# First block: values projected before the norm's statistics are known, projections woven between the softmax steps

## The chip, the cores and the metric

The kernel runs on one core of a Trainium2 chip. The metric is the device time of one execution in microseconds; three runs of the kernel before lie between 2774.18 and 2778.89, with a median of 2776.5.

## What is computed

The whole program is one hybrid block on 256 tokens of width 1024, followed by four further layers (gated linear attention, a conformer convolution, grouped-query attention, gated linear attention again), each with an MLP. The change lies at the very start of the first block. Cut to that part, the reference is:

```
xn = rmsnorm(x, norm1_w)                       # x * rsqrt(mean(x^2) + eps) * norm1_w
q, k, v, z, xbc, dt_raw, gate_logits = split(xn @ w_in)
# 24 heads of 64 in 3 dilated groups of 8, blocks of 128 queries, 256 keys
logits = q k^T / 8 + bias ;  masked where the key is out of the window
p = exp(logits - max) / sum                    # softmax; the 3 groups are merged
attn = p v                                     # by a softmax over all three together
merged = sigmoid(gate0) * (attn @ w_attn_branch) + sigmoid(gate1) * (ssm @ w_ssm_branch)
```

All arithmetic is float32. The weight products are made from three products each: a number is split into a rounded part "hi" and a rest "lo", and hi·hi, hi·lo and lo·hi are added up.

## The kernel before

**Weights.** Weights come in units. `Unit` loads a unit from HBM on SyncE's queue in chunks of 128x1024 floats (512 KB) into `wraw` (3 buffers), ScalarE rounds the chunk into `whi`, and VectorE takes the rest into `wlo` (5 buffers each, line 435). A projection (`fm2`) makes one unit of two chunks (four for the values) and then its 48 products through `mm3` (line 456): TensorE loads one operand and streams 256 columns of the other (512 for the values).

**Order.** The program is written as one sequence. A planner spreads it over the engines at build time. It keeps the written order where it can, but lets a later instruction go ahead on an engine when by its own estimates the earlier ones aren't ready. On the chip each engine then works its list strictly in that fixed order. So the load of the conditions (`conditions`, written after the keys) is issued at 9.18 us, and the sums of `decay_sums`, written after the fourth key unit, run between 28 and 52 us.

**Start.** x arrives, ScalarE squares it (line 408), VectorE adds the squares up, TensorE sums them over partitions with a matrix of ones (lines 523 and 524), and ScalarE and VectorE make the reciprocal root (`rstd_of`). After that x is normed and split into `h` (lines 545, 459, 460). Sixteen products with zeros (`warm`, line 417) run at the start and again while the root is made. `head_bias` makes the bias rows (line 615); `spread` later copies each row 128 times into a DRAM tensor `ud`, from which the skewed bias tiles `bt` are loaded (line 704).

**First projections.** `decays` takes one narrow unit (`dt`); three units of values follow, and six of keys. The queries are made just before the softmax step that needs them.

**Attention.** Eight steps follow, for four pairs of heads and two query blocks each. In a step `logits` multiplies queries and keys (lines 716, 720) and VectorE adds the bias; `soft` takes the maximum, the exponential and the sum, and VectorE multiplies the whole block by the reciprocal sum (line 736); `values` turns the block with TensorE (line 749: `T.transpose`, 72 in all), copies it out of PSUM and multiplies it with the values (line 755). `values` of a step is written after `soft` of the next one.

**After.** Four gate units `g0` alternate with products of the attention's output (`ab`), and then the state-space part begins.

PSUM has eight banks, three for projections (`pl`) and five for the rest (`pa`).

## Time and profile before

| | before |
|---|---|
| median of three runs | 2776.5 us |
| profiled execution: own time / span | 2776.37 us / 2774.6 us |
| TensorE busy | 98% of the span |
| VectorE, ScalarE, GpSimd busy | 77%, 46%, 8% |
| granted TensorE clock, mean | 0.989 |
| DMA | 420.40 MB, mean 152 GB/s |

The span is the time between the first and the last instruction that the profiler saw; all positions below are counted from its start. PE is TensorE, PEld its loading of the operand that stays, DVE VectorE, ACT ScalarE, POOL GpSimd, SP SyncE; a q behind the name is the engine's issuing of DMAs. The granted clock is 1.00 at 2.4 GHz and 0.50 at 1.2 GHz. A line number is that of the kernel before.

### The profile page before, as it was taken

The numbers are of one execution on the slowest core, as the hardware profiler recorded it, in microseconds if no ns is written. First come the engines' busy times: TensorE is split into PE (matmuls) and PEld (weight loads), VectorE is DVE, ScalarE is ACT, GpSimd is POOL, SyncE is SP. The second block draws the span as 40 slices with busy tenths as digits, with TensorE's granted clock in tenths as the row PEclk, the third lists the DMA queues.
The fourth block names the chain that finished last, engine by engine and source line by source line (L and its number), as shares of the span: only waits on it lengthen the run. The fifth ranks groups of instructions, "written<-read, shape, count | busy, mean of one in ns | idle before, by whom it ended". The sixth has DMA issues, their size and how long they took to land. (4 is left out here: it accounts for less than half of the span.)

```text
span 2774.6 us, 44026 instructions
## 1 busy us (share of the span) xinstructions
PE 2708.9 (98%) x17170; PEld 2375.0 (86%) x17170; DVE 2149.5 (77%) x3698; ACT 1272.9 (46%) x2225; POOL 216.5 (8%) x210
## 2 busy tenths in 40 slices
PE   8999999999999999999989999999999999999999
PEld 6889899999888888887668888897698888988999
DVE  6558987977886999657999996587699964754766
ACT  5455764445543522327655232245442323464543
POOL 0000100000000000003920000004600000000000
PEclk9999999999999999999999999999999999999999
DMA  6644466863443566333435663321156633222554
GB/s 229 226 146 159 142 224 220 288 206 125 139 145 114 168 213 207 110 101 97 130 122 168 213 211 120 97 84 46 54 167 212 211 108 103 90 80 83 179 184 140
DMA packets 122093, 420.40 MB, mean 152 GB/s; under 512 B 13201, under 2 KB 20108, under 8 KB 121756
## 3 DMA queue, kind: packets, MB, share of 16 engines
q1 hardware_dynamic: 114788, 402.45, 44.4%
q0 software_dynamic: 2080, 7.37, 0.8%
q10 hardware_dynamic: 5016, 7.76, 0.7%
q8 instruction: 135, 2.21, 0.3%
q14 instruction: 74, 0.61, 0.1%
HBM read 407.67 MB, written 5.84 MB: 149 GB/s over the span
## 5 line engine op out<-in xcount | busy, mean ns | idle before, releaser
L456 PE MATMUL pl<-hA,whi 128*128 128x256 f32 (+1 forms) x5056 | 1147.4, 321 | 9.4 <-ACT hA L459 3.6
L435 ACT CAST whi<-wraw 128x1024 fp32r<-128x1024 f32 x553 | 579.2, 1050 | 914.5 <-PE pl L456 379.4
L456 PEld LDWEIGHTS pl<-hA,whi 128*128 128x128 f32 x5056 | 845.0, 191 | 90.3 <-issue 5.6
L435 DVE TENSOR_TENSOR wlo<-wraw,whi 128x1024 fp32r<-128x1024 f32 x553 | 680.6, 1233 | 295.5 <-ACT whi L435 290.7
L456 PE MATMUL pl<-hA,wlo 128*128 128x256 f32 (+1 forms) x2528 | 805.5, 320 | 6.5 <-DVE wlo L435 6.3
L456 PE MATMUL pa<-oA,whi 128*128 128x512 f32 (+1 forms) x2592 | 640.3, 338 | 0.0
L456 PEld LDWEIGHTS pl<-hA,wlo 128*128 128x128 f32 x2528 | 481.1, 191 | 45.6 <-DVE wlo L435 9.3
L456 PEld LDWEIGHTS pa<-oA,whi 128*128 128x128 f32 x2592 | 447.4, 190 | 52.9
L564 DVE SCALAR_TENSOR_TENSOR mj<-mr,cs 128x1024 bf16<-128x1024 f32 x384 | 468.0, 1219 | 11.9 <-DMA mr<-in_wmod_dram 8.2
L456 PE MATMUL pa<-oA,wlo 128*128 128x512 f32 (+1 forms) x1296 | 438.0, 338 | 0.0
L1131 DVE SCALAR_TENSOR_TENSOR X<-pa,MOD,X 128x256 f32<-128x256 f32 x448 | 198.2, 478 | 106.7 <-PE pa L456 105.0
L456 PEld LDWEIGHTS pa<-oA,wlo 128*128 128x128 f32 x1296 | 245.9, 190 | 26.2
L456 PE MATMUL pl<-oA,whi 128*128 128x256 f32 (+1 forms) x1088 | 218.2, 299 | 11.3 <-ACT oA L459 11.3
L456 PE MATMUL pl<-whi,hA 128*128 128x256 f32 (+1 forms) x992 | 228.2, 321 | 0.4 <-DVE hA L1049 0.2
L456 PEld LDWEIGHTS pl<-oA,whi 128*128 128x128 f32 x1088 | 175.1, 193 | 18.8 <-ACT oA L459 12.2
L456 PEld LDWEIGHTS pl<-whi,hA 128*128 128x128 f32 x992 | 168.7, 195 | 13.1 <-DVE hA L1049 1.1
L456 PE MATMUL pl<-oA,wlo 128*128 128x256 f32 (+1 forms) x544 | 161.3, 298 | 0.0
L459 ACT CAST oA<-ct 128x256 fp32r<-128x256 f32 (+1 forms) x178 | 89.1, 506 | 155.3 <-DVE ct L1171 141.1
L456 PE MATMUL pl<-wlo,hA 128*128 128x256 f32 (+1 forms) x496 | 158.2, 320 | 0.0
L1746 POOL TENSOR_SCALAR pr<-pr,s 128x512 f32<-128x512 f32 (+1 forms) x64 | 78.5, 1245 | 499.5 <-DVE s L1744 499.2
L460 DVE TENSOR_TENSOR oA<-ct,oA 128x256 fp32r<-128x256 f32 (+1 forms) x178 | 96.4, 545 | 22.2 <-ACT oA L459 21.9
L456 PEld LDWEIGHTS pl<-oA,wlo 128*128 128x128 f32 x544 | 104.6, 193 | 2.5
(302 smaller groups left out, 2564.2 us busy)
## 6 DMA issues: line engine op xcount, KB each, us to landing
wraw<-in_wpk_dram SPq DMA_DIRECT2D x553, 512.0 KB, 4.1
mr<-in_wmod_dram SPq DMA_DIRECT2D x192, 512.0 KB, 4.4
U<-u SPq DMA_DIRECT2D x24, 265.5 KB, 4.9
ud<-rows ACTq DMA_DIRECT2D x3, 1536.0 KB
la<-lad POOLq DMA_DIRECT2D x8, 512.0 KB, 4.0
bt<-ud POOLq DMA_DIRECT2D x8, 384.0 KB, 6.8
U<-u SPq DMA_DIRECT2D x4, 273.5 KB, 5.2
U<-u SPq DMA_DIRECT2D x4, 269.5 KB
```

The lines of the kernel that those rows point to most:

```text
L435: i = A.copy(hi, raw).ins, V.tensor_tensor(lo, raw, hi, op=OP.subtract).ins
L456: T.matmul(o, l, r, start=ps.start(), stop=stop and i == 2)
L459: A.copy(hi, src)
L460: return V.tensor_tensor(lo, src, hi, op=OP.subtract).ins
L564: m = V.scalar_tensor_tensor(pool("mj", [P, D], BF), raw, 0.5, cs[:, s], op0=OP.mult, op1=OP.mult, accum_out=MOD[:, l, f, s:s + 1]).ins
L1131: V.scalar_tensor_tensor(X[:, k, c], ps, MOD[:, l, g + k, s:s + 1], X[:, k, c], op0=OP.mult, op1=OP.add)
L1746: G.tensor_scalar(pr, pr, dn[:, a:a + 1], None, op0=OP.mult)
```

## The change

The values are projected first, from x times the norm's weight (`xg`), chunk by chunk as the four pairs of x rows and the value weights arrive; the reciprocal root per token is applied when the result is copied out of PSUM. Only `norm1` is loaded ahead of the weights; the other vectors and constants follow after three chunks of values. `h` is made from the root while the second value unit runs. Each projection fetches and splits the next unit's weights before its own result is copied out (`ahead`, `nxt`). `dt` comes after the values. Then five units (keys 0 and 1, queries 0 and 1, keys 2) come ahead of the first softmax step, and the other units, two of the four gate units among them, are laid behind `soft` in the eight steps. Exponentials are no longer multiplied by the reciprocal sum; instead a 128x128 diagonal of it is made (`dg`), and a product of block and diagonal takes the place of each transpose. The bias rows are spread in four parts (two heads of each group) from GpSimd's queue instead of three parts from ScalarE's. The conditions and the sums of the decays move into steps 2 to 4. In the first block the second `warm` falls away. The ones are set by VectorE instead of being loaded.

```diff
+    ones = glob.tile([P, P], FT, name="ones")
+    V.memset(ones, 1.0)
...
+        def __init__(self, name, i, after=(), whole=True):
+            self.off, self.kt, self.cw = plan[name][i]
+            self.parts, self.raws = [], []
             last_unit[0] = self
+            for h in range(self.kt * self.cw // 1024 if whole else 0):
+                self.fetch()
+                self.cut(after[h] if after and isinstance(after[0], tuple) else after)
+        def fetch(self):
+            n, h = self.kt * self.cw, len(self.parts) + len(self.raws)
+            raw = glob.tile([P, 1024], FT, name="wraw", tag="wraw", bufs=WRAW)
+            self.dma = nc.sync.dma_start(raw, bass.AP(tensor=wpk.tensor, offset=wpk.offset + self.off + h * 1024, ap=[[n, P], [1, 1024]])).ins
+            self.raws.append(raw)
+        def cut(self, after=()):
+            raw = self.raws.pop(0)
+            hi = glob.tile([P, 1024], FR, name="whi", tag="whi", bufs=WHI)
+            lo = glob.tile([P, 1024], FR, name="wlo", tag="wlo", bufs=WHI)
+            i = A.copy(hi, raw).ins, V.tensor_tensor(lo, raw, hi, op=OP.subtract).ins
+            for a, b in zip(i, after):
+                if b is not None:
+                    order(a, b)
+            self.parts.append((hi, lo))
...
+    ready = {}
+    def ahead(name, i):
+        ready[name, i] = Unit(name, i)
+    def fm2(name, i, a, outer="f", after=(), nxt=None):
+        w = ready.pop((name, i), None) or Unit(name, i, after)
         ps = PL()
         order_ = [(k, f) for k in range(w.kt) for f in range(2)]
         if outer == "f":
             order_.sort(key=lambda x: x[1])
         for k, f in order_:
             mm3(ps, ps.t[:, f * 256:f * 256 + 256], w.at(k, f), a.at(k), k == w.kt - 1 and f == 1)
+        if nxt:
+            ahead(*nxt)
...
-            wide.append((ud[g * HPG:(g + 1) * HPG], rows))
-        def spread(after):
-            for dst, rows in wide:
-                i = nc.scalar.dma_start(dst, rows[:, None, :].to_broadcast([HPG, P, BW])).ins
-                order(i, after)
+            allrows.append(rows)
+        def spread(p):
+            for g, rows in enumerate(allrows):
+                nc.gpsimd.dma_start(ud[g * HPG + 2 * p:g * HPG + 2 * p + 2], rows[2 * p:2 * p + 2, None, :].to_broadcast([2, P, BW]))
...
-        w = Unit("dt", 0)
+        w = ready.pop(("dt", 0))
         ps = PL()
         for k in range(KD8):
             mm3(ps, ps.t[:, :256], w.at(k, 0), h.at(k), k == KD8 - 1)
+        ahead("k", 0)
...
-        pool.tags(k=6, bt=4, L1=4, L0=4, P1=2, P0=2, dt=5)
-        vt = [[O2([P, 512]) for _ in range(3)] for _ in range(2)]
-        for i in range(3):
-            w = Unit("v", i, () if i else norm_end)
-            ps = [PL() for _ in range(2)]
-            for k0 in range(0, KD8, 2):
-                for t in range(2):
-                    for k in (k0, k0 + 1):
-                        mm3(ps[t], ps[t].t, h.at(k, t * P, P), w.row(k), k == KD8 - 1)
-            for t in range(2):
-                A.copy(vt[t][i], ps[t].t)
+        def turn():
+            ps = PA()
+            for c in range(2):
+                T.transpose(ps.t[:, c * 32:c * 32 + 32], e[:, c * P:(c + 1) * P], ident[0:32, 0:32])
+                T.transpose(ps.t[:, 64 + c * 32:96 + c * 32], z[:, c * P:(c + 1) * P], ident[0:32, 0:32])
+            V.tensor_copy(tmv, ps.t[:, 0:128])
+        return turn
+    def attention(pool, h, vt, ud, spread, ab, late, gates):
+        pool.tags(k=6, bt=4, L1=4, L0=2, P1=2, P0=2, dt=5, dg=3)
         kf, qf = [], []
-        def proj(name, dst, i):
-            ps = fm2(name, i, h)
+        def proj(name, i, nxt=None):
+            if name == "g0":
+                gates(i, fm2(name, i, h, nxt=nxt))
+                return
+            ps = fm2(name, i, h, nxt=nxt)
             t = O2([P, 2, 256]) if name == "q" else pool(name, [P, 2, 256])
             A.copy(t, ps)
-            dst.append(t)
-        for i in range(6):
-            proj("k", kf, i)
-            if i == 0:
-                spread(last_unit[0].dma)
-            if i == 3:
-                late(pool)
+            (qf if name == "q" else kf).append(t)
...
-            for a, L in enumerate(Ls):
-                V.tensor_scalar(L, L, dn[:, a:a + 1], None, op0=OP.mult)
-        def values(p, qb, Ls):
+            dg = pool("dg", [P, 2, P])
+            for a in range(2):
+                V.tensor_scalar(dg[:, a], ident, dn[:, a:a + 1], None, op0=OP.mult)
+            return dg
...
-                        T.transpose(pt.t[:, b * P:b * P + P], Ls[a][:, (b0 + b) * P:(b0 + b) * P + P], ident)
+                        T.matmul(pt.t[:, b * P:b * P + P], Ls[a][:, (b0 + b) * P:(b0 + b) * P + P], dg[:, a], start=True, stop=True)
...
-        conditions(lambda: pool("P1", [P, 512], pad=[P, 768]))
-        mod_in(pool, MR[0])
+        first = [("k", 0), ("k", 1), ("q", 0), ("q", 1), ("k", 2)]
+        slots = [[("q", 2)], [("k", 3)], [("q", 3)], [("k", 4), ("q", 4)], [("k", 5)], [("q", 5)], [("g0", 0)], [("g0", 1)]]
         load_bias(0)
         load_bias(1)
-        done = 0
-        prev = None
+        for n, u in enumerate(first):
+            proj(*u, (first + slots[0])[n + 1])
+            if n == 0:
+                spread(1)
+        turn, prev = None, None
         for n, (p, qb) in enumerate(its):
-            need = (3 * p + 2) // 2 + 1
-            while done < need:
-                proj("q", qf, done)
-                done += 1
+            if n in (1, 3):
+                spread(n // 2 + 2)
             if qb and p + 1 < HPG // 2:
                 load_bias(2 * p + 2)
                 load_bias(2 * p + 3)
+            if n == 2:
+                turn = late(pool)
+            if n == 2:
+                load_conditions()
+            if n == 3:
+                mod_state["after"] = last_unit[0].dma
+                mod_in(pool, MR[0])
+            if n == 4:
+                conditions(lambda: pool("P1", [P, 512], pad=[P, 768]))
+                turn()
             Ls = logits(p, qb)
-            soft(Ls)
+            dg = soft(Ls)
+            for i, u in enumerate(slots[n]):
+                proj(*u, (slots[n] + slots[n + 1] if n + 1 < len(slots) else slots[n] + [None])[i + 1])
             if prev is not None:
                 values(*prev)
-            prev = (p, qb, Ls)
+            prev = (p, qb, Ls, dg)
...
+    def first_values(pool, hook):
+        x_ = lambda k: X[:, k, 0:256]
+        xg, h = Acts(256, "hA"), Acts(256, "hA")
+        vt = [[O2([P, 512]) for _ in range(3)] for _ in range(2)]
+        w = Unit("v", 0, whole=False)
+        for _ in range(3):
+            w.fetch()
+        nc.sync.dma_start(cst, cstd[:, 0:COFF["cos"][0]])
+        nc.sync.dma_start(vec[:, NV0:NVEC], vecd[:, NV0:NVEC])
+        acc = pool("ct", [P, 256], pad=[P, 512])
+        def part(w, ps, k0):
+            for t in range(2):
+                for k in (k0, k0 + 1):
+                    mm3(ps[t], ps[t].t, xg.at(k, t * P, P), w.row(k), k == KD8 - 1)
+        banks = [PA(), PA()]
+        for k0 in range(0, KD8, 2):
+            if k0 == 2:
+                w.fetch()
+            for k in (k0, k0 + 1):
+                hi, lo = xg.at(k)
+                A.activation(hi, x_(k), AF.Copy, scale=vv("norm1", k))
+                V.scalar_tensor_tensor(lo, x_(k), vv("norm1", k), hi, op0=OP.mult, op1=OP.subtract)
+            w.cut()
+            part(w, banks, k0)
+            for k in (k0, k0 + 1):
+                if k == 0:
+                    act(acc, x_(k), AF.Square)
+                    continue
+                q = ct(pool, 256)
+                act(q, x_(k), AF.Square)
+                V.tensor_tensor(acc, acc, q, op=OP.add)
+        ps = PL().t
+        T.matmul(ps[:, 0:256], ones, acc, start=True, stop=True)
+        for t in range(2):
+            T.matmul(ps[:, 256 + t:257 + t], acc[:, t * P:t * P + P], ones[:, 0:1], start=True, stop=True)
+        rt = rstd_small(ps[:, 256:258], D, 2)
+        r = rstd_of(pool, ps[:, 0:256], D, 256)
+        for i in range(3):
+            if i:
+                w = ready.pop(("v", i))
+                banks = [PA(), PA()]
+                for k0 in range(0, KD8, 2):
+                    part(w, banks, k0)
+            ahead(*(("v", i + 1) if i < 2 else ("dt", 0)))
+            for t in range(2):
+                A.activation(vt[t][i], banks[t].t, AF.Copy, scale=rt[:, t:t + 1])
+            if i == 0:
+                for k in range(KD8):
+                    f = ct(pool, 256)
+                    V.scalar_tensor_tensor(f, x_(k), vv("norm1", k), r, op0=OP.mult, op1=OP.mult)
+                    last = split(f, *h.at(k))
+                hold[:] = [last]
+                hook()
+        return h, vt
...
-            h = norm_plain(pool, lambda k: X[:, k, 0:256], "norm1", 256)
-            ud, spread = head_bias(pool)
+            bias = []
+            def rows():
+                bias.extend(head_bias(pool))
+                bias[1](0)
+            h, vt = first_values(pool, rows)
+            ud, spread = bias
             late, lad, dt_tm, la_tm = decays(pool, h)
         ab = Acts(256, "oA")
         with Pool("b1b") as pool:
-            attention(pool, h, ud, spread, ab, late)
+            mg = [X[:, 2 * i:2 * i + 2, 256:512] for i in range(4)]
+            gates = lambda i, ps: act(mg[i], ps, AF.Tanh, scale=0.5)
+            attention(pool, h, vt, ud, spread, ab, late, gates)
         with Pool("b1c") as pool:
-            mg = [X[:, 2 * i:2 * i + 2, 256:512] for i in range(4)]
             w = None
             for i in range(4):
-                ps = fm2("g0", i, h)
-                act(mg[i], ps, AF.Tanh, scale=0.5)
+                if i > 1:
+                    gates(i, fm2("g0", i, h))
...
-    nc.scalar.dma_start(vec, vecd[:, 0:NVEC])
-    nc.sync.dma_start(cst, cstd[:, 0:COFF["cos"][0]])
-    def conditions(th_):
+    nc.scalar.dma_start(vec[:, 0:NV0], vecd[:, 0:NV0])
+    if "b1" not in stages:
+        nc.scalar.dma_start(vec[:, NV0:NVEC], vecd[:, NV0:NVEC])
+        nc.sync.dma_start(cst, cstd[:, 0:COFF["cos"][0]])
+    def load_conditions():
```

## Rows read from the trace of the kernel before

**Rows 1.** The page: busy time, share of the span and instructions per engine.
```profile
PE 2708.9 (98%) x17170; PEld 2375.0 (86%) x17170; DVE 2149.5 (77%) x3698; ACT 1272.9 (46%) x2225; POOL 216.5 (8%) x210
```

**Rows 2.** Stretches: length, busy time per engine, granted clock, DMA share, GB/s.
```profile
0.00:10.00 10.00, 6.08 (x21) 2.69 (x22) 2.66 (x7) 4.15 (x10) 0.20 (x4) 1.00 0.77 247
10.00:20.00 10.00, 7.04 (x26) 3.19 (x25) 6.73 (x14) 6.91 (x14) 0.00 (x0) 0.87 0.85 319
18.42:24.12 5.70, 5.70 (x20) 5.12 (x21) 5.70 (x14) 4.50 (x10) 0.00 (x0) 0.50 0.23 77
18.42:120.00 101.58, 92.06 (x588) 83.27 (x589) 57.51 (x79) 46.74 (x62) 3.80 (x5) 0.94 0.69 232
116.06:119.87 3.81, 3.81 (x22) 3.41 (x23) 3.81 (x7) 0.31 (x1) 0.00 (x0) 0.51 0.66 227
120.00:182.00 62.00, 60.74 (x530) 51.98 (x529) 42.84 (x80) 32.29 (x66) 4.14 (x6) 1.00 0.36 119
182.00:220.00 38.00, 38.00 (x319) 38.00 (x318) 20.84 (x26) 25.23 (x44) 1.06 (x2) 1.00 0.59 201
```

**Rows 3.** The timeline of the start: start, duration, engine, line, idle before.
```profile
4.91 2.72 ACT L408 ACTIVATE ct<-X 128x256 f32<-128x256 f32 x8 [2.88 <-DMA X<-in_x_dram]
8.87 0.67 PE L523 MATMUL pa<-ct,cst 128*128 128x256 f32 x2 [2.93 <-DVE ct L528]
9.18 0.20 ACT L404 ACTIVATE s<-vec 32x1 f32<-32x1 f32 x1 [1.55 <-DMA vec<-in_vec_dram]
9.81 3.62 PE L417 MATMUL pa<-zero 128*128 128x512 bf16 x16
13.36 2.10 PE L615 MATMUL pa<-hot,vec 33*8 33x384 f32 x6
18.42 0.58 PE L456 MATMUL pl<-hA,whi 128*128 128x256 f32 x1 [2.96 <-ACT hA L459]
```

**Rows 4.** The waits of PE from 18.4 to 182: total, times, longest.
```profile
PE pl L720 <- ACT oA L687: 4.4, 2, 4.0
...
PE pl L456 <- ACT whi L435: 2.0, 1, 2.0
```

**Rows 5.** The timeline at the two long waits of PE.
```profile
57.81 6.03 ACTq L624 DMA_DIRECT2D ud<-rows  x1
63.88 0.59 ACT L687 COPY k<-pl 128x512 f32<-128x512 f32 x1 [4.62 <-PE pl L456]
64.37 1.99 ACT L435 CAST whi<-wraw 128x1024 fp32r<-128x1024 f32 x2
...
114.48 1.04 ACT L435 CAST whi<-wraw 128x1024 fp32r<-128x1024 f32 x1 [1.44 <-DMA wraw<-in_wpk_dram]
115.43 0.58 ACT L687 COPY oA<-pl 128x512 f32<-128x512 f32 x1
...
116.06 1.22 PE L720 MATMUL pl<-k,oA 64*128 64x256 f32 x4 [3.98 <-ACT oA L687]
```

**Rows 6.** The timeline of PE where plain products, transposes and weight products meet.
```profile
244.66 0.61 PE L832 MATMUL pa<-hA 128*128 128x128 f32 x4
...
245.10 1.04 PE L842 MATMUL pa<-cst,hA 128*128 128x128 f32 x8
...
245.89 0.48 PE L456 MATMUL pl<-hA,whi 128*128 128x256 f32 x2
```

**Rows 7.** Groups by line and form, 110 to 182 us: count, busy, mean ns.
```profile
L749 PE MATMUL pa<-cst,L 128*128 128x128 f32 x72 | 10.3, 278 | 0.8 <-DVE L L736 0.6
...
L736 DVE TENSOR_SCALAR L<-L,s 128x768 f32<-128x768 f32 x8 | 5.0, 663 | 0.0
```

**Rows 8.** Groups by line, 0 to 182 us: the rest "lo" of a chunk.
```profile
L435 DVE TENSOR_TENSOR wlo<-wraw,whi 128x1024 fp32r<-128x1024 f32 x43 | 52.3, 1223 | 56.8 <-ACT whi L435 56.8
```

**Rows 9.** DMA issues from 0 to 300 us: count, KB each, us to landing.
```profile
ud<-rows ACTq DMA_DIRECT2D x3, 1536.0 KB
bt<-ud POOLq DMA_DIRECT2D x8, 384.0 KB, 6.8
```

34 lines of the change are left out of this document (7 added, 27 removed).

## The prediction

> **What bounds the kernel now.** I read the page first: TensorE is busy for 2708.9 of 2774.6 us [rows 1], so the other engines matter only where TensorE waits for them, and 65.7 us of waiting is all there is to win. Then the table of stretches [rows 2]. From 182 on TensorE has no gap in 38 us. The time that the change can touch lies ahead of that: 18.4 us until the first weight product, 101.58 − 92.06 = 9.52 us of waiting between 18.42 and 120, and 62 − 60.74 = 1.26 us between 120 and 182. The same table shows two stretches at the lower clock level: 18.42 to 24.12 at 0.50 and 116.06 to 119.87 at 0.51. Both come right after TensorE had little or nothing to do. Half of each is lost: 5.70/2 + 3.81/2 = 4.76 us.
>
> Third the timeline of the start [rows 3]. x is there at 4.91, but the squares, the sum over partitions (from 8.87) and the root hold the first weight product back to 18.42; zeros and the bias rows (13.36 to 15.46) fill part of that. Fourth the waits of TensorE and what they are made of [rows 4, 5]. At 64 ScalarE's queue has been held for 6.03 us by the issue of the last `ud` copy; then comes the copy of the first keys, and only behind it the cast of the weights that TensorE wants next. At 116 it is the other way round: TensorE needs the second queries, whose copy stands behind a cast that waits for its DMA.
>
> So the place to win is 182 us long, and after it everything should move as one.
>
> **The sum: what stays.** I take the work that TensorE has done by 182.0 as a fixed set. From 18.42 that is 163.58 us, less 10.78 of waiting [rows 2] and 4.76 for the clock: 148.04 us of work at full clock.
>
> **Start of the values.** The first product now needs x times `norm1` and the first chunk. Four pieces of x (1.05 MB) and one chunk (0.52 MB) at the 247 to 319 GB/s of the first two stretches [rows 2] come to 6.4 us, or 2.2 us of silence and then 4.9: about 7 us, an estimate. One cast and one subtraction follow, 1.04 and 1.22 us [rows 5, 8], with latency to 9.6 us. A chunk feeds 12 products of 512 columns; 16 of that width take 3.62 us in the second set of zeros [rows 3], so a chunk lasts 12 × 0.226 = 2.7 us. Chunks two and three arrive at some 9 and 11 us and are ready in time. The fourth needs the first buffer back and stands behind constants and vectors (0.73 MB): 3.87 MB by about 14.4 us, split by 17.7. The first unit ends near 20.6 with 11 us of work done, as if work had begun at 9.6 without a gap.
>
> **What is added to TensorE.** The bias rows lay in the gap ahead of 18.42; now they lie in the stream: 2.1 us [rows 3]. The sum over partitions is now one product of 256 columns and two of one column; two of 256 took from 8.87 to the zeros at 9.81, 0.94 us [rows 3], and I take 0.9. The second set of zeros lay in the gap and saves nothing.
>
> The large item is the diagonal. 72 transposes [rows 7] become 72 plain float32 products. The nearest rows are exact in shape: two plain products of 128x128 by 128x128 appear as four instructions and start at 244.66, the eight transposes behind them at 245.10, the next weight product at 245.89 [rows 6]. That is 0.44/2 = 0.22 us for a product and 0.79/8 = 0.10 to 0.11 for a transpose. The change costs 72 × 0.11 = 7.9 us of TensorE. What it saves is VectorE's: 8 multiplications of 663 ns [rows 7] and 8 of half that width become 16 narrow ones, some 5 us, on an engine that isn't the bound here.
>
> The Trainium skill speaks against this edit: "Perfetto Trace Analysis", section Transposes, says to use the transpose rather than a standard matmul. "FP8 and Floating Point Precision", section TensorE Precision Notes, has true float32 in four passes through the array; the row shows two instructions. By four passes of 0.11 a product would take 0.44, the edit 72 × 0.33 = 23.8 us, and the sum would end 15.9 us later; the row decides for two.
>
> **What is moved at no cost.** The two gate units cost the same wherever they lie. The extra split of x (eight casts, eight subtractions) lies beside weight-bound products; without that cover it would be under 8 us of VectorE. The sums of the decays and the conditions lie on VectorE beside attention's products. Between 120 and 182 TensorE did 60.74 us, four query units of 48 × 0.119 = 5.7 us among them (319 instructions in 38 us from 182 on [rows 2]); attention's own part is then some 35, and with nine units between its steps 87. VectorE was busy for 42.84 of 62 us there; ten more subtractions add 12.2 [rows 8], and if sums and conditions add as much again, it is 67 of 87. Spreading the bias in quarters from GpSimd frees ScalarE of the 6.03 us hold [rows 5]. On GpSimd's queue the bias loads stand behind it. `ud` is 4.7 MB in all and a bias load takes 6.8 us to land [rows 9]; with copy, landing and two loads at some 17 us for each pair of heads, in series from 27 us, the pairs are there at 44, 62, 79 and 97, and are wanted from about 77, 99, 121 and 143: hidden by over 30 us. If that cover were gone, each pair would hold TensorE for what is missing.
>
> **The sum.** 9.6 + 148.04 + 7.9 + 2.1 + 0.9 = 168.54, against 182.0: 13.46 us earlier if nothing waits. What will wait can't be read off the trace of before, so I bound it. The clock at the start: 0 if TensorE is granted the full clock at 9.6, as at 9.81 after a similar gap (16 products in 3.62 us [rows 3]), or 2.85 as at 18.42; I take 1.4. Handing over after the first unit: the copies need a root of six small steps, bias rows and second unit share five banks; 0 to 3, I take 1. The five units ahead of the first softmax step: 0 if fetching ahead ends both long waits, 9.5 if they come back; since both causes are edited away [rows 5], 1.5. Softmax steps with units between them: 0 to 2.5; 2, since 1.26 us were left there with fewer units. That makes 5.9, and a gain of 7.5 us. The profiled execution took 2776.37, 0.1 under the median, so the changed kernel should take 2769.0. Bounds: no waits at all gives 2763, all of them 17.85 − 13.46 = 4.4 us more than before, 2780.8.
>
> **Rivals.**
> *Nearly no wait is left* (under 2 us): both long waits have one cause each, and the units between are ready ahead of need. 2762 to 2765.
> *New waits take the place of the old.* ScalarE and VectorE work strictly in order, and the start now rests on them. The exponential of `a_log`, written far later, was set early and waited 1.55 us for the vectors [rows 3]; these now come behind three chunks, near 13 us, and would hold the casts of the values. Such a hold of 3 to 4 us, with the waits above at their middle, leaves a gain of 0 to 5: 2771 to 2776.
> *The product with the diagonal costs more than its row*, and the kernel gets slower. From 0.325 us each the gain is gone: 72 × (0.325 − 0.11) = 15.5 = 13.46 + 7.9 − 5.9. If it took four instructions of 0.11 instead of two, the time would be 2785. The row says two for the same shape [rows 6]. The page on precision named above is what speaks for four.
> *The lower clock stays through all of the values*, since gaps between chunks interrupt them: 33 us of products at half speed add up to 33, less the 1.4 taken already. That would be slower from 9 us of such work on, and slower by 5.5 from 14.5. Against it: in before the clock rose after 5.7 us of unbroken work [rows 2].
>
> **Chances.** One measurement of this kernel tells 0.2%, 5.5 us. The forecast, a gain of 5.5 to 11 us, gets 0.43; nearly no wait 0.16; new waits with an end within 5.5 us of before 0.28; the dear diagonal 0.05; the clock 0.05; other ways to be slower 0.03. Faster 0.59, same 0.28, slower 0.13. The range for 8 in 10 reaches from all but no waits, 2762, to all of the bounds at once, 2780; the forecast's own is 2765 to 2771.
>
> **What would show it.** First weight product at 9 to 10 us and the first value unit done by 20 to 23. 144 instructions where 72 transposes were, some 0.11 us apart. No copy into `ud` on ScalarE's queue, and waits of TensorE of 2 to 6 us where 10.8 were. The last product of the attention's output some 7 us earlier, and the same distance kept to the end. It is wrong if TensorE waits for more than 8 us between 20 and 175, if the clock is 0.50 for more than 6 us ahead of 30, or if the gain at 220 isn't that at the end.

## The result and the profile after

The changed kernel takes 2808.1 us (median of four runs, 2806.1 to 2809.8), against 2777.2 for the kernel before on the same chip: a ratio of 1.0115, with a 95% interval of 1.0102 to 1.0128. The forecast was 2769, a gain. The change costs 31 us.

The page of the profiled execution (2808.71 us, span 2806.9) shows TensorE busier than before [rows 1], and yet later:

```profile
PE 2723.5 (97%) x17228; PEld 2389.1 (85%) x17228; DVE 2149.9 (77%) x3712; ACT 1277.2 (46%) x2235; POOL 231.1 (8%) x222
```

The last of the four gate residuals that VectorE adds to X after the attention (line 951 before, 1042 after) is a landmark: it starts at 210.26 before and at 241.71 after. The 31.45 us between them are the whole loss; from there to the end both kernels take as long, within 1 us. The table of stretches (columns as in [rows 2]) shows where it arises:

```profile
9.55:23.82 14.27, 12.23 (x54) 9.86 (x55) 9.60 (x16) 8.02 (x15) 0.00 (x0) 1.00 0.89 318
23.82:32.00 8.18, 6.50 (x15) 3.26 (x16) 6.68 (x15) 7.22 (x16) 0.00 (x0) 0.58 0.47 153
32.00:84.00 52.00, 51.82 (x348) 47.69 (x346) 31.43 (x49) 23.89 (x32) 13.03 (x13) 1.00 0.81 238
84.00:100.00 16.00, 6.39 (x35) 5.09 (x34) 4.90 (x4) 5.15 (x6) 0.00 (x0) 0.69 0.71 235
100.00:117.00 17.00, 13.68 (x101) 12.03 (x101) 7.84 (x10) 5.15 (x6) 0.00 (x0) 0.90 0.39 133
117.00:182.00 65.00, 57.18 (x437) 50.95 (x435) 31.56 (x57) 26.90 (x47) 6.84 (x8) 0.92 0.40 123
```

The start does what it was built for: the first weight product stands at 9.55 instead of 18.42 [rows 3], as the timeline has it. From 23.82 to 32 TensorE then loses 1.7 us idle and 2.7 to the clock, and from 32 to 84 it has next to no gap.

```profile
9.55 0.73 PE L468 MATMUL pa<-whi,hA 128*128 128x512 f32 x2 [3.04 <-ACT hA L979]
```

Then it works for 6.4 of 16 us, partly at the lower clock, and until 182 it loses a little in every stretch, where before it lost 1.26 us from 120 to 182 [rows 2].

I split the way to the landmark into 1 us stretches: what is not busy is idle, busy time times (1 − granted clock) is lost to the clock, and the rest is work. Before, from 18.42: idle 10.8, clock 4.8, work 176.3. After, from 9.55: 27.6, 12.8 and 191.8. So −8.9 for the start, +15.4 of work, +16.9 of idle time, +8.0 of clock. The waits of TensorE up to the landmark, longest first, answer to [rows 4]:

```profile
PE pl L729 <- ACT oA L705: 8.2, 3, 5.2
PE pl L468 <- ACT k L705: 6.2, 3, 4.4
PE pa L468 <- ACT hA L979: 3.0, 1, 3.0
PE pl L729 <- DVE L L735: 3.0, 3, 1.0
```

And the timeline of the worst place, by engine, answers to [rows 5] (`...` marks rows left out):

```profile
85.31 1.04 ACT L447 CAST whi<-wraw 128x1024 fp32r<-128x1024 f32 x1 [3.57 <-DMA wraw<-in_wpk_dram]
89.54 1.04 ACT L447 CAST whi<-wraw 128x1024 fp32r<-128x1024 f32 x1 [3.19 <-DMA wraw<-in_wpk_dram]
90.49 0.58 ACT L705 COPY oA<-pl 128x512 f32<-128x512 f32 x1
...
91.12 1.23 PE L729 MATMUL pl<-k,oA 64*128 64x256 f32 x4 [5.18 <-ACT oA L705]
96.78 0.80 PE L468 MATMUL pl<-hA,whi 128*128 128x256 f32 x2 [4.43 <-ACT k L705]
...
112.83 1.23 DVE L447 TENSOR_TENSOR wlo<-wraw,whi 128x1024 fp32r<-128x1024 f32 x1 [1.65 <-ACT whi L447]
113.98 0.68 DVE L732 SCALAR_TENSOR_TENSOR L<-pa,bt 128x512 f32<-128x512 f32 x1
114.58 0.41 DVE L735 SCALAR_TENSOR_TENSOR L<-pl,bt 128x256 f32<-128x256 f32 x1
114.91 1.14 DVE L732 SCALAR_TENSOR_TENSOR L<-pa,bt 128x384 f32<-128x384 f32 x2
115.97 0.41 DVE L735 SCALAR_TENSOR_TENSOR L<-pl,bt 128x256 f32<-128x256 f32 x1
```

Two things are to be seen. Casts wait for weights that have not landed, and the copy that TensorE needs stands behind them: it is the second wait of [rows 5] again. And the logits that TensorE wrote to two of the three `pl` banks at 91 to 92 get their bias only at 114.58 and 115.97: in VectorE's fixed order eight subtractions of later units stand ahead, each waiting for its cast. Until then one bank is left for all projections. The same pattern comes back, smaller, at 113 to 117, 142 to 153, 179 to 182 and 206 to 214.

### The profile page after: what moved, and what is told of

It reads as the page before. It is cut to its first block, busy times and chain, and to the rows that moved or that the text cites. A ratio compares the mean times of both kernels' runs of the same rounds, so it can differ in the third digit from the quotient of the medians.

```text
span 2806.9 us, 44171 instructions
## 1 busy us (share of the span) xinstructions
PE 2723.5 (97%) x17228; PEld 2389.1 (85%) x17228; DVE 2149.9 (77%) x3712; ACT 1277.2 (46%) x2235; POOL 231.1 (8%) x222
## 5 line engine op out<-in xcount | busy, mean ns | idle before, releaser
L468 PE MATMUL pl<-oA,whi 128*128 128x256 f32 (+1 forms) x1088 | 220.7, 302 | 13.2 <-ACT oA L471 11.3
L468 PE MATMUL pl<-whi,hA 128*128 128x256 f32 (+1 forms) x896 | 197.4, 313 | 0.3
L468 PEld LDWEIGHTS pl<-whi,hA 128*128 128x128 f32 x896 | 150.7, 195 | 9.3 <-DVE hA L1140 0.7
L468 PE MATMUL pl<-wlo,hA 128*128 128x256 f32 (+1 forms) x448 | 139.4, 312 | 0.0
## 6 DMA issues: line engine op xcount, KB each, us to landing
ud<-rows POOLq DMA_DIRECT2D x12, 384.0 KB, 16.9
```

The lines of the kernel that those rows point to most:

```text
L468: T.matmul(o, l, r, start=ps.start(), stop=stop and i == 2)
```

## The experiments

Each is told by its change to the changed kernel unless another is named; in the cuts of code, `...` marks what is left out. "Landmark" is the place above. Ratios are to the kernel before, 2777 us, so 0.001 is 2.8 us; ± about 0.0015.

### Diagonal, queue, or the start itself?

**e1_transposes.**
```diff
-            dg = pool("dg", [P, 2, P])
-            for a in range(2):
-                V.tensor_scalar(dg[:, a], ident, dn[:, a:a + 1], None, op0=OP.mult)
+            for a, L in enumerate(Ls):
+                V.tensor_scalar(L, L, dn[:, a:a + 1], None, op0=OP.mult)
...
-                        T.matmul(pt.t[:, b * P:b * P + P], Ls[a][:, (b0 + b) * P:(b0 + b) * P + P], dg[:, a], start=True, stop=True)
+                        T.transpose(pt.t[:, b * P:b * P + P], Ls[a][:, (b0 + b) * P:(b0 + b) * P + P], ident)
```


> The changed kernel with one part undone: the probabilities are scaled by VectorE and turned by transposes as in the kernel before, instead of a product with a diagonal of the reciprocals. Theory 1 (the added work is what the prediction priced, and the loss is waits that stand elsewhere): TensorE's busy time in the turns falls by about 7 us (144 products at 0.117 against 72 transposes of two halves at the old busy time, 17.5 against 10.3), the waits of 5.2 and 4.4 us near 91 and 97 us stay, time 2799 to 2803. Rival (the diagonal makes VectorE and TensorE wait for each other at each softmax, so that it carries most of the loss): 2790 or less, and the waits near 113 to 117 us go with it.

Measured: 2802.0, 1.0094; landmark 234.29, work 6.8 us less, idle time about the same (28.1 against 27.6). The long waits stay. The groups by line, first of the changed kernel, then of this run, show the price, as the row of two plain products had it [rows 6, 7]:

```profile
L761 PE MATMUL pa<-dg,L 128*128 128x128 f32 x144 | 17.5, 276 | 0.8 <-DVE dg L746 0.8
```
```profile
L759 PE MATMUL pa<-cst,L 128*128 128x128 f32 x72 | 10.1, 275 | 0.7 <-DVE L L745 0.7
```

The diagonal is worth 6 (by the ratios) to 7 (by the landmark) of the 31 us, and the long waits don't come from it.

**e2_sync_queue, e2_scalar_queue.**
```diff
-                nc.gpsimd.dma_start(ud[g * HPG + 2 * p:g * HPG + 2 * p + 2], rows[2 * p:2 * p + 2, None, :].to_broadcast([2, P, BW]))
+                nc.sync.dma_start(ud[g * HPG + 2 * p:g * HPG + 2 * p + 2], rows[2 * p:2 * p + 2, None, :].to_broadcast([2, P, BW]))
```


> The changed kernel with the four quarters in which the bias rows are spread issued by SyncE's queue instead of GpSimd's; nothing else is edited. Theory 1 (the bias chain on GpSimd's queue is counted as late when the order of VectorE's instructions is laid out, so that the first bias additions stand behind eight subtractions of later units and two of three PSUM banks are held from 91 to 114 us): in this kernel's order the first additions stand behind 20 subtractions of the start of the run instead of 32, the waits of 5.2 and 4.4 us go, idle time of TensorE before the fourth gate residual falls from 27.6 to 10 to 17 us, and the time to 2785 to 2797. Rival A (the copies behind the casts in ScalarE's order make the waits, whatever the bias does): under 4 us gained, 2804 to 2812. Rival B (the spread's transfers ahead of the weights on the same queue hold the weights up): slower, 2812 to 2830.

> The same edit with ScalarE's queue, where the weights' transfers are not in the same queue; first bias additions behind 23 subtractions instead of 32. Theory 1: as with SyncE's queue, 2785 to 2797, a little above it where the issue of a quarter blocks ScalarE. Rival A: 2804 to 2812. Rival B expects this one to be faster than the one on SyncE's queue by the time that the weights were held up there.

Measured: 2830.4 (1.0193, landmark 268.35) and 2810.9 (1.0126, landmark 245.86). Theory 1 missed both times, though the waits of 5.2 and 4.4 us went. On SyncE's queue the result is the one rival B had, 0.4 us above its range. On ScalarE's the time lies in rival A's range, but not by its cause, since TensorE's waits for copies fall from 16.7 us to 1.5; the timeline shows what happens when further transfers are issued while the first are under way:

```profile
35.08 0.70 ACTq L645 DMA_DIRECT2D ud<-rows  x1
36.09 9.91 ACTq L645 DMA_DIRECT2D ud<-rows  x2
46.63 11.30 ACTq L645 DMA_DIRECT2D ud<-rows  x1
```

Behind each such issue, of 9.91 and 11.30 us, the casts wait. So these two say little of the first theory: each pays on its own queue.

**e4_start** (the kernel before with the start alone)
```diff
+            h, vt = first_values(pool, rows)
...
+            attention(pool, h, vt, ud, spread, ab, late)
```
(with `attention` and `head_bias` as before but for the values, and `load_conditions` ahead of `conditions`)

> One half of the change alone: the first block begins with the values (weights prefetched, sums of squares beside the products, scale on the copies), but the attention is the one of the kernel before: all units of the keys first, one spread of the bias by ScalarE's queue, decay sums with their transposes at the fourth unit, queries on demand, transposes, the four gate units behind the attention. Theory 1 (the start is sound, gains about 9 us ahead of the first key unit and keeps most of it; the whole loss is in the turns): 2767 to 2773. Rival (the start only moves the wait: the later units then wait for weights, for the clock or for the bias, as in the changed kernel): 2775 to 2785, not faster than before.

Measured: 2775.6, 1.0001 (0.9992 to 1.0010); landmark 209.50. The rival was right. The 8.8 us of the start are given back: 2.4 as work (bias rows and sums now lie in the stream), 1.1 idle, 4.5 clock. The waits of TensorE:

```profile
PE pa L688 <- DVE dt L676: 4.4, 1, 4.4
PE pa L468 <- ACT hA L970: 3.1, 1, 3.1
PE pl L468 <- ACT whi L447: 2.1, 1, 2.1
PE pa L468 <- ACT u L637: 2.0, 1, 2.0
```

**e6_mended_start** (e4_start with)
```diff
-            ps = PA()
+            ps = PL()
             T.matmul(ps.t[0:HPG, :BW], vec[0:33, o:o + HPG], hot, start=True, stop=True)
...
-                late(pool)()
+                turn = late(pool)
+            if i == 5:
+                turn()
```


> The start alone as in the run before (2775.6 us, where its 8.8 us were given back as 2.4 of work, 1.1 of idle time and 4.5 of low clock), with two of its three waits taken away: the products for the bias rows write to the other PSUM pool, so that the second value unit does not wait 2.04 us for the copy of the row, and the transposes of the decay sums come two units later, so that TensorE does not wait 4.43 us for them. Theory (each wait costs itself and the half clock after it): 6.5 us of waits and about 4.3 us of low clock come back, landmark 8 to 11 us earlier, time 2764 to 2768. Rival (the waits move to the next late thing): 2772 to 2777.

Measured: 2768.2, 0.9973 (0.9964 to 0.9982), landmark 202.03: the time is 0.2 us over the theory's range, the landmark 7.5 us earlier where it had 8 to 11. Half of the change, mended at two places, beats the kernel before.

### The bias spread, or the turns?

**e5_no_spread** (the spread is left out, and the bias tiles hold other values)
```diff
-            nc.gpsimd.dma_start(bt, bass.AP(tensor=row.tensor, offset=row.offset + 128, ap=[[BW - 1, P], [HPG * P * BW, 3], [1, 256]]))
+            nc.gpsimd.dma_start(bt, wmod[0, hh, :, 0:768].rearrange("p (g k) -> p g k", g=3))
...
-            for g, rows in enumerate(allrows):
+            for g, rows in enumerate(()):
```


> The changed kernel without the spread of the bias rows: its twelve transfers are left out, and the bias tiles are filled by the same number of loads of the same size from the modulation weights, so that they wait for no transfer; the bias values are other ones. Theory 1 (the spread by GpSimd's queue, in packets of under 512 bytes and in a chain with the loads, makes most of the waits between 80 and 118 us: it holds up the weights and the order puts the first bias additions late): idle time ahead of the fourth gate residual falls from 27.6 to under 14 us, clock loss from 12.8 to under 8, and the time to 2781 to 2790. Rival (the turns by themselves make the waits, by copies that stand behind casts in ScalarE's order): idle stays over 22 us, time 2798 or more.

Measured: 2765.4, 0.9961 (0.9948 to 0.9975), landmark 197.65, idle 1.7, clock 3.4. This is 43 us less than the changed kernel, far more than theory 1 expected. All the waits of TensorE that the view lists up to the landmark:

```profile
PE pa L468 <- ACT hA L978: 3.4, 1, 3.4
PE pa L468 <- ACT u L637: 1.3, 1, 1.3
PE pa L419 <- DVE zero L414: 1.1, 1, 1.1
```

Start, turns, fetching ahead and diagonal together cost no wait after 84 us once the spread is gone.

**e7_one_spread.**
```diff
             for g, rows in enumerate(allrows):
-                nc.gpsimd.dma_start(ud[g * HPG + 2 * p:g * HPG + 2 * p + 2], rows[2 * p:2 * p + 2, None, :].to_broadcast([2, P, BW]))
+                i = nc.scalar.dma_start(ud[g * HPG:(g + 1) * HPG], rows[:, None, :].to_broadcast([HPG, P, BW])).ins
+                order(i, p)
```
(called once, after the first key unit; the first two bias loads behind it; the three transfers are of 1536 KB each, and not of the 1152 of the expectation)

> The changed kernel with the bias spread as in the kernel before: three transfers of 1152 KB on ScalarE's queue after the first key unit, instead of twelve of 384 KB on GpSimd's; the turns and the diagonal stay. Theory 1: most of what leaving the spread out gives, since the packets are whole rows again; 2784 to 2795, the first bias additions behind 28 subtractions. Rival A (any spread beside the turns holds the weights up): 2800 to 2812. Rival B (copies behind casts): 2800 to 2808, with the waits for the copies still over 12 us.

Measured: 2774.2, 0.9995 (0.9985 to 1.0004), landmark 209.39: 33 us of the 43 come back, and the time is below what was expected. One long wait is left, behind four bias loads that are issued at once among the weights; that these make it is argued from their place alone:

```profile
86.62 3.25 POOL L714 DMA_DIRECT2D bt<-ud  x4 [86.18 <-DVE dt L674]
...
92.76 0.58 PE L468 MATMUL pl<-hA,whi 128*128 128x256 f32 x1 [8.01 <-ACT k L706]
```

**e3_copy_dve.**
```diff
-            A.copy(t, ps)
+            V.tensor_copy(t, ps)
```


> The changed kernel with the copies of the key and query units from PSUM made by VectorE instead of ScalarE, nothing else. Rival B of the runs before (the head of ScalarE's order: each copy stands behind casts that wait for weights or for buffers, so that a PSUM bank is held): the waits for the copies, 15.9 us in three groups, fall by 8 us or more and the time to 2785 to 2797. Theory 1 (the weights are late, and the copies only show it; VectorE's copies stand behind subtractions that wait for the same casts): under 4 us either way, 2802 to 2811, the waits now named after VectorE.

Measured: 2803.3, 1.0100, landmark 237.07; idle 25.6 instead of 27.6, the waits named after VectorE (6.2 for k, 4.5 for oA). That is what theory 1 had: the copies show the wait, and moving them doesn't end it. VectorE's copies stand behind subtractions that wait for the same casts, so copies with nothing ahead of them were not tried.

### Traffic, order, or the chain of loads?

**e5b_spread_unread, e5c_packets_only** (the twelve transfers stay; the bias tiles come from elsewhere, with other values)
```diff
-            nc.gpsimd.dma_start(bt, bass.AP(tensor=row.tensor, offset=row.offset + 128, ap=[[BW - 1, P], [HPG * P * BW, 3], [1, 256]]))
+            nc.scalar.dma_start(bt, wmod[0, hh, :, 0:768].rearrange("p (g k) -> p g k", g=3))
```
(`nc.gpsimd` in e5b)

> The changed kernel with all twelve transfers of the spread as they are, but with the bias tiles filled from the modulation weights, so that no load waits for the spread (other bias values). The order of the engines stays that of the changed kernel: the first bias additions behind 32 subtractions. Theory 1a (the small packets hold the weights up) and theory 1b (the late place of the additions in VectorE's order holds two PSUM banks) both expect little change, 2798 to 2811; theory 1c (the loads themselves wait for the spread and come too late) expects most of the 42 us that leaving the spread out gave: 2765 to 2780.

> The same, but the bias tiles are loaded by ScalarE's queue; the twelve transfers stay on GpSimd's queue, unread, with their small packets. With the loads out of GpSimd's queue the order becomes that of the kernel without a spread: the first bias additions behind 28 subtractions. Theory 1a (small packets): 2790 to 2808, the casts wait for weights between 80 and 96 us as before. Theory 1b (order of the additions): 2764 to 2775, nearly the 2765.4 of the kernel without a spread. In between: both carry part.

Measured: e5b 2803.9, 1.0093, landmark 238.37; e5c 2792.1, 1.0047, landmark 210.16. In the changed kernel's order it costs little that the loads wait for the spread, 3.3 us at the landmark, and 1c falls as it stood. With the same transfers, e5c reaches the landmark 28 us earlier than e5b; it has the better order, but also another queue for its loads. Its total lies in the range of 1a. But it loses 17 us behind the landmark, in the state-space part, which the planner also laid out otherwise, so its total is no price of the traffic.

**e8_pool_one** (e7_one_spread with `nc.gpsimd` for `nc.scalar`), **e9_combo** (e7_one_spread with the edits of e1 and the `PL` of e6)

> The kernel with one spread after the first key unit (2774.2 us on ScalarE's queue), its three transfers of 1.5 MB on GpSimd's queue instead. Theory 1a (GpSimd's queue cuts them into packets of under 512 bytes, whoever waits): 2790 to 2810. Theory 1d (it was the cutting into twelve pieces, which take a turn of the queue each, and not the queue): 2770 to 2780.

> What the runs speak for, together: the changed kernel's start and turns, one spread on ScalarE's queue after the first key unit, transposes instead of the diagonal, and the bias rows' products in the other PSUM pool. From the 2774.2 us of the kernel with one spread: transposes -6.8 of work, the wait of 2.06 us at 25.7 and the half clock after it -3; 2764 to 2768, below the kernel before by 0.3 to 0.45%. Rival (the one wait of 8 us behind the four bias loads grows by what is gained ahead of it, since the spread lands when it lands): 2770 to 2776.

Measured: e8 2781.9, 1.0013 (1.0003 to 1.0023), landmark 213.06: slightly over theory 1d, far under 1a. Three transfers on GpSimd's queue cost 0.0018, 5 us, more than on ScalarE's; the changed kernel with its twelve lies 33 us above e7, its other order included. The DMA issues of the two, the changed kernel's first, from 30 us on:

```profile
ud<-rows POOLq DMA_DIRECT2D x9, 384.0 KB, 17.5
```
```profile
ud<-rows POOLq DMA_DIRECT2D x3, 1536.0 KB, 16.2
```

A quarter of the bytes takes as long to land.

e9: 2771.5, 0.9977 (0.9967 to 0.9987), landmark 205.00, as the rival had it: the wait behind the four loads stayed at 8.2 us.

What the transfers do to the weights shows in the DMA view from 78 to 92 us, of the changed kernel and of e5_no_spread:

```profile
DMA packets 2129, 3.66 MB, mean 261 GB/s; under 512 B 1253, under 2 KB 1253, under 8 KB 2129
...
q0 software_dynamic: 1481, 1.32, 35.0%
...
wraw<-in_wpk_dram SPq DMA_DIRECT2D x5, 512.0 KB, 5.9
```
```profile
DMA packets 532, 1.93 MB, mean 138 GB/s; under 512 B 64, under 2 KB 64, under 8 KB 531
...
wraw<-in_wpk_dram SPq DMA_DIRECT2D x4, 512.0 KB, 3.4
```

GpSimd's queue (q0) takes a third of the DMA engines' time, most of its packets are under 512 bytes, and a chunk of weights lands in 5.9 us instead of 3.4.

### The order by itself

**e12_adds_first.**
```diff
-        ready[name, i] = Unit(name, i)
+        ready[name, i] = Unit(name, i, (None, adds[-1]) if adds else ())
```
(`adds` holds the last bias addition of each step with 256 keys)

> The changed kernel with one thing added to VectorE's order: the subtractions of the units that are fetched after a step's logits come behind the bias additions of that step, so that the first additions stand behind 25 subtractions instead of 32. The spread's twelve transfers, their queue, their small packets and the bias loads stay as they are. Theory 1b (the place of the additions in the order holds the PSUM banks and makes most of the loss): landmark of the fourth gate residual at 205 to 215 us instead of 241.7, time 2771 to 2783. Theory 1a (the small packets, which hold the weights up, make most of it): landmark over 228, time 2794 or more.

Measured: 2812.0, 1.0126, landmark 241.38. Theory 1b missed as it stood, and the numbers are those that 1a had. This tells little, though: the waits for copies fell (8.2 to 4.8 and 6.2 to 3.7), but TensorE now waits 15.7 us for subtractions (line 447), which stand behind additions that wait for the logits. I had moved the wait, not removed it. Two instructions can't be exchanged in a fixed order without looking at all of it, so the next runs fix all of it.

**e11_big_rows** (the same twelve transfers, but of whole rows from other weights, so that the bias values are others)
```diff
-                nc.gpsimd.dma_start(ud[g * HPG + 2 * p:g * HPG + 2 * p + 2], rows[2 * p:2 * p + 2, None, :].to_broadcast([2, P, BW]))
+                dst = ud[g * HPG + 2 * p]
+                nc.gpsimd.dma_start(bass.AP(tensor=dst.tensor, offset=dst.offset, ap=[[1024, 96], [1, 1024]]), wmod[0, g * 4 + p, 0:96])
```
**e14_early_order, e15_late_order** (the changed kernel with the order of e11, and e11 with the order of the changed kernel; instructions are numbered as written, and `LAID` lists their numbers, engine by engine, as the other kernel has them)
```diff
+        for l in LAID.values():
+            last = None
...
+                    if last is not None:
+                        order(i, last)
+                    last = i
```


> The changed kernel; each of the spread's twelve transfers still moves 384 KB by GpSimd's queue into the same memory, and the bias loads still wait for it, but the source is a contiguous piece of the modulation weights instead of a row repeated 128 times (other bias values). In the laid-out order the first bias additions then stand behind 28 subtractions instead of 32, as in the kernels with one spread. Theory (the loss comes by the repeated rows, through traffic or through the order): 2764 to 2776. Rival (twelve transfers and the chain of loads behind them on one queue are the cause, whatever the rows are): 2790 or more.

> The changed kernel with nothing moved in memory: same twelve transfers with repeated rows, same queue, same waits of the loads. Only the order of the instructions of TensorE, VectorE and ScalarE up to the end of the attention is fixed to be that of the run with whole rows. Order theory (the late additions and the two steps laid together make the loss that comes back in each pair of heads, some 20 us between the 504th and the 792nd weight product): that stretch takes 58 to 63 us instead of 79.7, time 2778 to 2792; what stays above the run with whole rows is what the traffic costs. Traffic theory: the stretch stays over 72 us, time 2797 or more.

> The other corner: whole rows as in the run with contiguous pieces, and the order of the three engines fixed to that of the changed kernel. Order theory: the stretch between the 504th and the 792nd weight product takes 76 to 86 us, time 20 to 30 us above the run with whole rows and its own order, 2786 to 2802. Traffic theory: within 8 us of that run.

Measured, as ratio, landmark, and the stretch from the start of the 504th to that of the 792nd weight product, counted one by one (the 79.7 of the expectations was a miscount):

| | early order | late order | order costs |
|---|---|---|---|
| repeated rows | e14: 1.0046, 221.40, 60.5 us | the change: 1.0115, 241.71, 83.1 us | 0.0069 |
| whole rows | e11: 1.0005, 211.00, 60.6 us | e15: 1.0070, 230.92, 80.1 us | 0.0065 |

The order costs 18 to 19 us by the times and 20 by the landmarks, with either traffic, as the order theory had it; e15 is 18.9 us above e11, where it had 20 to 30, and e11 itself (2776.7, e14 2788.6, e15 2795.6) is 0.7 us over its range. In this stretch the repeated rows cost nothing in the early order (60.5 against 60.6) and 3 us in the late one. In the timeline of TensorE the third pair of heads shows it, first of the changed kernel, then of e14:

```profile
142.47 0.51 PE L468 MATMUL pl<-hA,whi 128*128 128x256 f32 x2 [1.55 <-ACT k L705]
...
149.99 0.70 PE L729 MATMUL pl<-k,oA 64*128 64x256 f32 x2 [1.50 <-ACT oA L705]
151.70 1.22 PE L729 MATMUL pl<-k,oA 64*128 64x256 f32 x2 [1.01 <-DVE L L735]
153.09 0.80 PE L468 MATMUL pl<-hA,whi 128*128 128x256 f32 x2 [0.17 <-DVE L L735]
```
```profile
141.79 1.14 PE L368 MATMUL pa<-k,oA 64*128 64x256 f32 x8
142.76 0.60 PE L368 MATMUL pl<-k,oA 64*128 64x256 f32 x4
143.29 0.51 PE L368 MATMUL pl<-hA,whi 128*128 128x256 f32 x2
```

4.2 us of waits for a bank, and behind them products at the lower clock (0.80 us where 0.51 is usual; the granted clock is 0.50 from 152 to 158), against none. (In e14 and e15 all instructions carry the line of a helper.)

The rows of the table differ by 0.0041 to 0.0045, 12 us, but that is not all of the traffic: the whole rows wait for no bias row, so they are moved in the first 30 us, among x and the first weights, where the 144th weight product comes 11 to 13 us later (63.8 and 62.8, against 51.3 and 51.7). With those back the traffic costs some 24 us, an estimate. From e5_no_spread to e14 it is measured: 1.0046 − 0.9961 = 0.0085, 23.6 us. The order has no part in this: up to the landmark TensorE works the same list in e5_no_spread, e11 and e14, and in the lists of the other two engines only one pair of casts and of subtractions, at 168 us, stands elsewhere in e14. By the split, order (e14 to the change) is 9.7 us idle, 2.9 clock and 7.7 work, and traffic (e5_no_spread to e14) 16.2, 6.4 and 1.1.

**e13_early_spread** (e8_pool_one with the edits of e1, e6's `PL` and e12), **e16_pool_laid** (the same without e12's, in the order of e9)

> A version made of what the runs showed: the changed kernel's start and turns; the spread in three transfers of 1.5 MB, all on GpSimd's queue at the start, so that the bias tiles are loaded near 62 us and not in one lot near 85; the additions ahead of later units' subtractions; transposes instead of the diagonal; the bias rows' products in the other PSUM pool. From the 213.1 us of the kernel with three transfers on GpSimd's queue: transposes -6.8, wait for the bias row's copy with the half clock after it -3.5, its waits of 7.6 us for copies and additions with their clock -9; landmark 192 to 198, time 2756 to 2763. Rival (the small packets of three transfers still hold weights up, and the waits only change names): 2767 to 2775.

> A version to beat both: the changed kernel's start and turns, transposes, bias rows' products in the other PSUM pool, the spread in three transfers of 1.5 MB on GpSimd's queue at the start (so that the first four bias loads stand near 62 us and not near 85), and the order of the three engines fixed to that of the 2771.5 us version. That version lost 8.2 us in one wait behind the four late loads. Order theory: this wait goes or falls under 3 us, landmark 192 to 200, time 2756 to 2765. Rival (the small packets of the early spread cost what is gained): 2768 to 2778.

Measured: e13 2777.7, 1.0006 (0.9997 to 1.0015), landmark 210.01; e16 2772.3, 0.9986 (0.9977 to 0.9995), landmark 206.56. e16's rival was right; e13 ended 2.7 us above even its rival. In e16, with the bias loads at 64 and the good order, TensorE still waits 4.4 us at 92.06, and from 30 us to the landmark casts wait 25.9 us for weights, against 11.2 in e5_no_spread. From 40 to 64 us, beside the spread, a chunk of weights takes 9.7 us to land; that this delay is what TensorE pays at 92, when the spread has long landed, is argued. Neither beats e6_mended_start; it, e9_combo and e16_pool_laid are the versions with the whole bias that lie below the kernel before, by 0.14 to 0.27%.

## Why the prediction was wrong

**The step that failed** is the one that priced the spread at nothing, and with it the 1.5 us for waits that were to be edited away. Of the spread the prediction says: "in series from 27 us, the pairs are there at 44, 62, 79 and 97 … hidden by over 30 us". GpSimd's timeline shows the loads later than I had them:

```profile
53.58 1.58 POOL L713 DMA_DIRECT2D bt<-ud  x2 [14.88 <-DMA ud<-rows]
55.15 3.22 POOL L645 DMA_DIRECT2D ud<-rows  x3
77.40 1.57 POOL L713 DMA_DIRECT2D bt<-ud  x2 [19.03 <-DMA ud<-rows]
```

But VectorE's waits up to the landmark name no bias tile. The cover held, and the spread cost 43 us (e5_no_spread against the changed kernel), in two ways that "hidden" doesn't count:

- Traffic, some 24 us. Casts wait for late weights (37.0 us up to the landmark in e14, 18.0 in e5_no_spread), and copies that free a bank stand behind the casts. I weighed only when the bias would arrive, not what its 4.7 MB do to what else is under way. [rows 9] gave no landing time for a copy into `ud`; my 17 us for a pair left some 10 for its copy, and that took 17.5 by itself.
- Order, 18 to 19 us. The planner lays out every engine's list by its own estimates. With twelve transfers of repeated rows in the queue ahead of the loads it put the first additions behind 32 subtractions instead of 28, laid two steps' logits together, and kept this up for all four pairs. e14 and e15 show what the whole order costs; the place of the first additions alone isn't it, since e8_pool_one too has them behind 32 and takes 67.0 us for the stretch of the table. That the estimate of GpSimd's queue is the cause is argued from e5b and e5c, where moving only the loads to another queue gives one order or the other.

How much of the 24 is packets alone and how much the loads' waiting for the spread stays open: by landmarks 12.5 and 11.2 us in the early order (e5, e5c, e14), but 3.3 for the waiting in the late one (e5b), and e5c also changed the loads' queue.

**The other steps.** The start was right: 9.55 us for the first product, and the first unit done by 20.96, when the sum over partitions starts. The diagonal was priced at 7.9 and measured 6.8. Bias rows and sums: 3.0, measured 2.4.

The "five units ahead of the first softmax", 1.5 of at most 9.5, took the 5.2 and 4.4 us seen at 91 and 97, about the 9.5 that it gave "if they come back". The reason for taking 1.5, that both causes of [rows 5] were edited away, was wrong for the second: since the next unit is split ahead of a unit's own copy, the copies of keys and queries stand right behind two casts of the next unit, in ScalarE's list of the changed kernel and of e5_no_spread alike. So in the timeline of e5_no_spread:

```profile
89.34 1.98 ACT L447 CAST whi<-wraw 128x1024 fp32r<-128x1024 f32 x2
91.22 0.57 ACT L705 COPY oA<-pl 128x512 f32<-128x512 f32 x1
```

What e5_no_spread took away is the lateness of the weights, and there this order cost nothing; a copy written ahead of the casts was not tried.

The allowances of 5.9 us in all stand against 1.7 idle and 3.4 clock in e5_no_spread, and its 2765.4 against the 2769.0 forecast: the sum comes out near the change without its spread. In part that is luck, since the work grew by 6.7 us there where the sum had 10.9. Of the 15.4 us of work added in the changed kernel, 7.7 go with the late order, since e14 shows 184.0 us of work. Twenty more weight products than before lie ahead of the landmark, 2.1 us; seven of them go with the late order, some 0.7, and the rest of its 7.7 I can't place. The other 7.7 should be 6.8, 2.4 and 1.4 for thirteen products, 10.6 in all, so this count of work is no better than some 3 us.

Attention's own part between 120 and 182 was misread: 60.74 less four units of 5.7 is 38 and not 35, which changes no term of the sum.

**The rivals.** "New waits take the place of the old" named the right kind of thing at the wrong place (the start) and for the wrong price (0 to 5 us of gain left). The diagonal at four instructions and the clock through all values didn't come. The dear diagonal had been priced at four times 0.11 us, but the 16 bf16 products of 512 columns in 3.62 us [rows 3] make 0.057 for 128 columns, and four of those are 0.23, an estimate, about the 0.22 that its row had for a product: four passes and two instructions don't contradict each other here, and the 2785 had no ground. Of the signs given for a failure one came: TensorE waits for 21.3 us between 20 and 175, over the 8 named. The clock was at 0.50 from 25.2 to 32, of which 4.8 us lie ahead of 30, under the 6 named, and the distance at the landmark was the one at the end.

Two rules of the Trainium skill bear on this. "Perfetto Trace Analysis", section Transposes, prefers the transpose to a standard matmul; e1_transposes agrees, by 6.8 us of work. The other speaks of the spread: "DMA: Bandwidth & Descriptors", section Rules for kernel authors, says that an outermost dimension of fewer than 16 confines a transfer to as many engines. Pieces with 2 outermost landed in 17.5 us and pieces of four times the bytes with 8 outermost in 16.2, which fits; on how many engines either ran no view here shows, and a spread with the 128 rows outermost was not tried.

## What to carry to other kernels

A transfer that is hidden for its reader isn't free: price what it takes from the transfers that the bound engine lives on, and test it by leaving it out, which here told more than any edit of its queue. Where a planner lays out the order, any edit of one queue is also an edit of the order of all engines; take the order of the one kernel into the other before you call it traffic. And a wait named after a copy or an addition is often only the head of a fixed list: follow it to what stands ahead.

## What was not expected of the hardware

A DRAM-to-DRAM copy of repeated rows takes 17.5 us to land for 384 KB and 16.2 for 1536 KB from GpSimd's queue. From 30 us to the landmark, on all queues, 8368 packets are under 512 bytes with the twelve small ones, 2031 with the three large and 957 without a spread. Issued one behind the other on ScalarE's queue, such copies held that engine's issue for 9.9 to 11.3 us, while GpSimd issued each in about 1.1. And waits of TensorE bring the lower clock with them: the changed kernel lost 12.8 us to it beside 27.6 idle, while e5_no_spread, which has no wait after 84, loses nothing to it there (all of its 3.4 lie ahead).
